# The last piece of the Fourier weight fold ahead of the last two gate blocks, and the output weights of the even layer split by GpSimd

## The chip, the cores and the metric

The kernel runs on one core of one Trainium2 chip. The metric is the device time of one launch in microseconds. Its matmuls run on PE (TensorE, with PEld for its weight loads), and DVE, ACT and POOL are VectorE, ScalarE and GpSimd. SP issues most of the DMAs, and POOL issues some.

## The reference

One inference step of a two-layer backbone over 1280 tokens of width 1024, 1024 latent and 256 context tokens. Cut to what the change touches:

```python
# layer 0 (even): two attention mixers (8 heads of 64 each) and a SiLU gate for each
qa, ka, va, ga, qb, kb, vb, gb = split_even(h @ w_in)
oa = attention over all latent and context keys
ob = attention over a window of +-128 tokens and the context keys, with a sink
x = x + gate * (concat([oa * silu(ga), ob * silu(gb)]) @ w_out)
# layer 1 (odd): Fourier mixing, also gated
u, g = split(modulate(rms_norm(x)) @ w_in1)
x = x + gate * ((real(fft2(u, axes=(positions, group channels))) * silu(g)) @ w_out1)
y = rms_norm(x)
```

The channel half of the Fourier transform of one group is a product with a fixed matrix. The kernel multiplies it into the odd layer's input weights instead of applying it to the tokens; this product of two weights is the *fold*, in four groups f0 to f3.

## The kernel before, in words

**Arithmetic.** The tokens are ten tiles of 128 (0 to 7 latent, 8 and 9 context). Each fp32 operand of a projection is held as a high and a low part of the type fp32r, high = the rounded value and low = value minus high, and a product is three matmuls (`mm3`). `split` makes the two parts: one engine copies the high part, another then subtracts. The letters "a", "d" and "p" in its arguments name ACT, DVE and POOL, and a longer string such as "pd" is a cycle.

**Stages.** First the modulation vectors, the normalised tokens and the folds f0 to f2; then the projections of layer 0; then attention, from about 240 us of the span to about 800; then the output projection of layer 0, the norm, and layer 1. Attention runs in units (tile, key group, head pair), which `attend` walks. One unit computes scores (`soft`: sC against context keys, sB against the window, sL against all latent keys), takes maxima on DVE, exponentials on ACT, transposes the probabilities on PE (pt), splits them with an ACT copy (L277) and a DVE subtraction (L1048), and multiplies by the values (`weigh`: av). When the last key group of a tile t is done, `totals` makes its softmax denominators (tt, stored in scd). Outputs go to DRAM (od).

**The filler.** A unit leaves PE idle while ACT and DVE work. So the rest of layer 0 is put into one queue of pieces with a cost each (`Filler`), and after each unit `attend` pumps as many pieces as the unit's budget pays for: 2.9 us for a unit of the windowed mixer. In the queue, by `ORDER`: the remaining q and k/v blocks, then the SiLU gate blocks g0 to g3. The last two of these are run together, by token group: ga40, ga50, ga60, ga70, then ga41 and so on up to ga72 (the digits are column block and token group). Between these pieces stand the splits of the output weights (`wout_next`), eight blocks of 128 rows, each in two halves: a load on SP (`sp.dma_start`, L1107) into a raw tile of the zone h, the high part by ACT (E_WO "a", L277), the low part by POOL and DVE in turn (L283), each 128x512. A half needs the raw tile until its low part is done; zone h has nine tiles, which the gates use too. After the gates come: the load of the fold f3 (two tiles of zone w, 512 KB each, and the fixed matrix, 256 KB), the loads of the first output projection's inputs (`load_to(0)`), the four fold pieces (wa30 to wa33: eight matmuls L559 each, into the one PSUM bank "g", out of it by an ACT copy, stored to wd by SP), and then the ten steps of the output projection (oz), each preceded by its loads. A gate block uses the same bank "g", and frees it when the tanh (L817) and the DVE operations behind it have read it.

**Inputs of the output projection.** `proj_in` loads od, gd (the stored gates), scd (denominators) and the residual x from POOL's own DMA queue while attention runs, and from SP's afterwards. It multiplies od, gd and scd together (L1221, L1222, on POOL while attention runs, on DVE afterwards) and splits the product (ACT, then DVE). After a step comes `proj_step`: the residual is added, the squares are summed by ACT (L1344), the token rows normalised (p, L1370) and transposed (eoE, L1274).

**Order.** The program text gives the dependences; the instructions of each engine are then laid out in the order of the framework's own timeline, so that a change in one place moves rows of every engine behind it. Only SP's order in the first phase is written by hand.

Of the kernel before, what the change touches and what calls it, by code (L numbers as in the profile page):

```python
# [24 lines left out]
UV = ("u",)  # L25
FILL_A, FILL_B, LAG_A, LAG_B = 4.4, 2.9, 1, 2
E_PH, E_OH, E_OL, E_WO = "a", "a", "d", "a"
# [30 lines left out]
FC, XF = 1.3, False  # L58
# [2 lines left out]
PAIRS = ((0, 4), (2, 6), (3, 7), (1, 5), (8, 9))  # L61
FILL_C, NLATE = 2.9, 8
E_FQ, E_GD = "d", "d"
ORDER = "qa0 qa1 kb0 qb0 qb1 g0 g1 g2 g3"
FLATE = "f3"
AT_B = "s"
AT_F = (0, 1, 2)
AT_N, AT_Z = (0, 0, 3, 0, 3, 2, 2, 2, 2, 2, 3, 3, 3), ("p", "pt", "q")
# [71 lines left out]
def hybrid_step(ctx: ExitStack, tc: tile.TileContext, I, O):  # L140
# [140 lines left out]
    def split(dst_h, dst_l, src, hc="a", lc="p"):  # L281
        copy("hi" + hc, hc, dst_h, src)
        pick("lo" + lc, lc).tensor_sub(dst_l, src, dst_h)  # L283


    def load_w(src, width=256, tags="w", gap=None, lc=E_WL, each=None, later=None):
        out = []
        for kp in range(2):
            hi = take(tags, (P, 4, width), F32R)
            lo = take(tags, (P, 4, width), F32R)  # L290
            for j in range(2):
                r0 = (kp * 4 + j * 2) * P
                if width <= 256:
                    raw = take("h", (P, 2, width))
                else:
                    raw = take(("p", "pt", "q", "w"), (P, 2, width))
                if gap is None:
                    sp.dma_start(raw.a, src[r0 : r0 + 2 * P, :].rearrange("(j p) f -> p j f", p=P))
                else:
                    gap(raw, r0)  # L300
                if each is not None:
                    each(raw, kp * 4 + 2 * j)

                def fin(raw=raw, hi=hi[:, 2 * j : 2 * j + 2, :], lo=lo[:, 2 * j : 2 * j + 2, :]):
                    split(hi, lo, raw.a, XE["wh"], lc)
                    drop(raw)

                if later is None:
                    fin()
                else:  # L310
                    later.append(fin)
            out.append((hi, lo))
        return out
# [11 lines left out]
    def w0cols(c0):  # L325
        return I["w_in0"][:, c0 : c0 + 256]
# [209 lines left out]
    def fold_load(g, parts=1):  # L536
        if "f" not in fold:
            fold["f"] = take("h", (P, 2, 256))
            sp.dma_start(fold["f"].a, I["fch"])
        wu = [take("w", (P, 1024)) for j in range(2)]  # L540
        for h in range(parts):
            cols = slice(h * (1024 // parts), (h + 1) * (1024 // parts))
            for j in range(2):
                sp.dma_start(wu[j][:, cols], I["wuT"][(2 * g + j) * P : (2 * g + j + 1) * P, cols])
        return wu
# [7 lines left out]
    def fold_piece(g, kb2, wu, first=False):  # L553
        f = fold["f"]
        acc = bank("t" if first else "g", f"wa{g}{kb2}")
        for i in range(2):
            c0 = (2 * kb2 + i) * P
            for j in range(2):
                pe.matmul(  # L559
                    acc[:, i * 256 : i * 256 + 256], wu[j][:, c0 : c0 + P], f[:, j, :], start=j == 0, stop=j == 1  # L560
                )
        if first:
            if kb2 % 2 == 0:
                early[g, kb2 // 2] = take("u", (P, 4, 256))
            wo = early[g, kb2 // 2][:, 2 * (kb2 % 2) : 2 * (kb2 % 2) + 2, :]
        else:
            wb = take("h", (P, 2, 256))
            wo = wb.a
        copy("wo", "a", wo, acc.rearrange("p (i f) -> p i f", i=2))
        if not first:  # L570
            fold_put(g, kb2 * 256, wo)
            drop(wb)
        if kb2 == 3:
            drop(*wu)
            fold["n"] = fold.get("n", 0) + 1
            if fold["n"] in (EF, 4):
                drop(f)
                del fold["f"]
# [265 lines left out]
    fl_ = Filler()  # L844
    fl_.depth = 9
    ws = {}
# [250 lines left out]
                after(u0)  # L1097
            fl_.pump(budget(un))

    def out_weights(src, ks, tags, lc="pd"):  # L1100
        out = []
        for k in ks:
            hi, lo = take(tags, (P, D), F32R), take(tags, (P, D), F32R)
            for hf in range(2):
                raw = take("h", (P, 512))
                sl = slice(hf * 512, hf * 512 + 512)
                sp.dma_start(raw.a, src[k * P : (k + 1) * P, sl])  # L1107
                split(hi[:, sl], lo[:, sl], raw.a, E_WO, lc)
                drop(raw)
            out.append((hi, lo))  # L1110
        return out
# [3 lines left out]
    wout = []  # L1115
    ws["qa0"] = wqa0

    def loader(nm):
        def fn():
            ws[nm] = load_w(w0cols(base[nm[:-1]] + 256 * int(nm[-1])))  # L1120
            return 0
        return fn
# [11 lines left out]

    def wout_next(n):
        for _ in range(n):
            fl_.add(0.0, lambda k=wk_left.popleft(): wout.extend(out_weights(I["w_out0"], (k,), UV)) or 0)

    for i, nm in enumerate(order[:-1]):
        j = int(nm[-1])  # L1140
        work = []
        if nm[0] == "q":
            m = "ab".index(nm[1])
            for t in range(0, NT, 2):
                if nm == "qa0" and t in (0, 2):
                    continue
                work.append((5.4, lambda t=t, nm=nm, m=m, j=j: q_pair(m, j, t, ws[nm], "g"), ("q", t, 2 * m + j)))
        elif nm == "kb0":
            for t in range(0, NT, 2):
                work.append((5.4, lambda t=t, nm=nm: kv_pair(1, t, ws[nm], "g"), ("kb", t)))  # L1150
        elif i < len(order) - 2:
            work += [gate_work(j, c, gi) for c in range(2) for gi in range(3)]
        if i > 0:
            fl_.add(0.0, loader(order[i + 1]))
        for w in work:
            fl_.add(*w)
        if i < len(order) - 2:
            fl_.add(0.0, releaser(nm))

    for gi in range(3):  # L1160
# [223 lines left out]
    def can_run(i, j):  # L1384
        r = pairs[i][j]

        def fn():
            if sum(len(spare[z]) for z in OB[0]) < NSP or i > EARLY:
                return False
            return all(finished.get(t, 99) + SPAN < clock[0] for t in USES[r])  # L1390
        return fn
# [5 lines left out]
    def load_to(n):  # L1397
        while loaded[0] <= min(n, 9):
            proj_load(*steps[loaded[0]])
            loaded[0] += 1  # L1400
        return 0


    def late_fold(nm):
        def fn():
            ws[nm] = fold_load(int(nm[1]))
            return 0
        return fn

    for n, nm in enumerate(FLATE.split()):  # L1410
        fl_.add(0.0, late_fold(nm))
        if n == 0:
            fl_.add(0.0, lambda: load_to(0), ready=can_run(0, 0))
        for k in range(4):
            fl_.add(FC, lambda k=k, nm=nm: fold_piece(int(nm[1]), k, ws[nm]))
    if not FLATE:
        fl_.add(0.0, lambda: load_to(0), ready=can_run(0, 0))
    for n, ij in enumerate(steps):
        if n == 8:
            fl_.add(0.0, lambda: wgs.append(load_w(I["w_g1"][:, 0:256], tags=BIG)) or 0)  # L1420
# [413 lines left out]
    hi, lo, xr = ins1  # L1834
# [133 lines left out]
```

## Time and profile before

| what | us |
|---|---|
| runs of the kernel, median (lowest to highest) | 1191.62 (1185.96 to 1196.26) |
| the profiled execution: span from its first to its last instruction | 1196.9 |
| PE busy in the span | 1159.1 |
| DVE busy | 834.5 |
| ACT busy | 577.1 |
| POOL busy | 286.0 |
| moved by DMA | 168.81 MB |

The profile is one execution, here one that took 5.3 us more than the median of the runs; everything between the first and the last instruction is in its span, and nothing is known of what lies around it. Rows of the waits give engine, operation and line, what ended the wait, and then total idle us, count, and median. In rows of the timeline the first number is the time in the span and the second the duration, and the brackets hold the idle time ahead and what ended it. The granted clock is the share of full clock that PE was given, 0.50 being half.

### The profile page before, as it was taken

What the parts mean: (1) busy time and instruction counts of PE and PEld (TensorE: products, weight loads), DVE (VectorE), ACT (ScalarE), POOL (GpSimd) and SP (SyncE); (2) the same over time, 40 slices, a digit from 0 to 9 for tenths busy, and PEclk for the clock granted to TensorE, in tenths of its full rate; (3) what the DMA queues carried; (4) which work ended last, traced back from release to release, by engine and by line L of the source; (5) the groups of instructions that cost most, each with busy time, mean ns of one, the idle gap of its engine ahead of it and who ended that gap; (6) DMA issues with size and microseconds to landing.
All of it is one profiled execution on the core that took longest, in us unless ns stands there. A gap on an engine that the chain in (4) does not pass through costs nothing.

```text
span 1196.9 us, 22002 instructions
## 1 busy us (share of the span) xinstructions
PE 1159.1 (97%) x8103; PEld 1037.9 (87%) x8103; DVE 834.5 (70%) x2006; ACT 577.1 (48%) x1159; POOL 286.0 (24%) x272
## 2 busy tenths in 40 slices
PE   8999999999999999999999989998999999999997
PEld 6788899999999998899888878886878888998886
DVE  2489778787777776678888867777755964367543
ACT  4442555555656655556676654532364225333211
POOL 2255644512222230011010035200212226200001
PEclk9999999999999999999999989998998999999999
DMA  9978512323532232444354477774214435364321
GB/s 327 365 257 272 160 59 69 89 77 113 148 89 78 76 95 84 100 120 116 83 148 105 131 223 203 232 224 160 85 45 136 147 115 167 109 186 150 141 105 54
DMA packets 130096, 168.81 MB, mean 141 GB/s; under 512 B 26298, under 2 KB 86454, under 8 KB 129988
## 3 DMA queue, kind: packets, MB, share of 16 engines
q1 hardware_dynamic: 127476, 158.74, 43.5%
q0 software_dynamic: 2368, 8.39, 2.3%
q8 instruction: 64, 1.05, 0.4%
q14 instruction: 44, 0.36, 0.1%
q10 hardware_dynamic: 144, 0.26, 0.1%
HBM read 123.19 MB, written 44.16 MB: 140 GB/s over the span
## 4 chain that ended last, share of the span: by engine, by line
PE 80%; DMA 9%; DVE 5%; ACT 2%; issue 2%; SPq 1%; POOL 1%; POOLq 0%; DVEq 0%; ACTq 0%
PE of L265 9%; PE q L265 8%; PE av L1051 8%; PE pt L1045 8%; PE ga L265 7%; PE sL L928 5%; PE u L265 5%; PE oz L265 4%; PE g1E L265 4%; PE g1O L265 4%; PE kv L265 3%; PE sC L928 2%; PE wa L559 2%; PE g1c L265 2%; DMA h<-i_w_out 2%
## 5 line engine op out<-in xcount | busy, mean ns | idle before, releaser
L277 ACT ACTIVATE pt<-pt 128x512 fp32r<-128x512 f32 (+1 forms) x265 | 146.8, 575 | 107.0 <-PE pt L1045 60.2
L1048 DVE TENSOR_TENSOR pt<-pt,pt 128x512 fp32r<-128x512 f32 (+1 forms) x264 | 170.8, 658 | 37.7 <-ACT pt L277 36.8
L1051 PE MATMUL av<-pt,u 128*128 128x256 f32 x1008 | 167.1, 289 | 0.7 <-ACT pt L277 0.7
L1045 PE MATMUL pt<-identr,p 128*128 128x128 f32 x1008 | 157.4, 273 | 1.1 <-ACT p L969 0.8
L265 PE MATMUL q<-w,u 128*128 128x256 f32 x960 | 143.9, 287 | 0.0
L1051 PEld LDWEIGHTS av<-pt,u 128*128 128x128 f32 x1008 | 138.9, 190 | 4.6 <-ACT pt L277 0.9
L265 PEld LDWEIGHTS q<-w,u 128*128 128x128 f32 x960 | 126.8, 188 | 4.9 <-issue 0.8
L1045 PEld LDWEIGHTS pt<-identr,p 128*128 128x128 f32 x1008 | 119.7, 141 | 8.0 <-ACT p L969 1.0
L969 ACT ACTIVATE p<-p,nm 128x1280 f32<-128x1280 f32 (+1 forms) x80 | 95.5, 1194 | 63.1 <-DVE p L962 62.8
L265 PE MATMUL ga<-u,w 128*128 128x512 f32 (+1 forms) x576 | 124.1, 360 | 0.8 <-DVE byp L1024 0.5
L265 PEld LDWEIGHTS ga<-u,w 128*128 128x128 f32 x576 | 93.6, 188 | 15.2 <-ACT pt L277 1.2
L283 POOL TENSOR_TENSOR w<-h,w 128x512 fp32r<-128x512 f32 x38 | 51.1, 1360 | 143.4 <-DVE w L279 115.0
L928 PE MATMUL sL<-u,q 128*128 128x512 f32 x256 | 82.4, 411 | 2.0 <-DMA q<-qd 2.0
L969 ACT ACTIVATE p<-p,NM 128x640 f32<-128x640 f32 (+2 forms) x80 | 59.2, 740 | 39.5 <-DVE p L962 39.4
L928 PE MATMUL sC<-u,q 128*128 128x256 f32 x320 | 61.8, 294 | 1.6 <-DMA q<-qd 1.0
L962 DVE TENSOR_SCALAR_CACHE_REDUCE p<-sL 128x512 f32<-128x512 f32 x64 | 43.9, 685 | 23.2 <-PE sL L928 14.2
L962 DVE TENSOR_SCALAR_CACHE_REDUCE p<-sL,nm 128x512 f32<-128x512 f32 x64 | 47.7, 745 | 13.7 <-PE sL L928 12.9
L265 PE MATMUL oz<-u,w 128*128 128x512 f32 x192 | 57.3, 403 | 0.0
L283 POOL TENSOR_TENSOR u<-h,u 128x512 fp32r<-128x512 f32 x16 | 20.6, 1293 | 138.0 <-ACT u L277 133.9
L928 PEld LDWEIGHTS sC<-u,q 128*128 128x128 f32 x320 | 48.8, 189 | 5.5 <-issue 1.1
L265 PE MATMUL oz<-u,u 128*128 128x512 f32 x160 | 48.7, 405 | 4.0 <-ACT u L277 2.5
L702 POOL TENSOR_TENSOR h<-h,rope 128x512 f32<-128x512 f32 (+1 forms) x18 | 21.9, 1214 | 126.4 <-ACT h L785 80.5
(728 smaller groups left out, 2569.8 us busy)
## 6 DMA issues: line engine op xcount, KB each, us to landing
q<-qd SPq DMA_DIRECT2D x80, 256.0 KB
h<-i_w_in SPq DMA_DIRECT2D x40, 256.0 KB
p<-i_ada_w SPq DMA_DIRECT2D x18, 512.0 KB
h<-i_w_out SPq DMA_DIRECT2D x32, 256.0 KB
pt<-i_ada_w SPq DMA_DIRECT2D x15, 512.0 KB
qd<-pt SPq DMA_DIRECT2D x20, 256.0 KB
q<-i_ada_w SPq DMA_DIRECT2D x9, 512.0 KB
qd<-q SPq DMA_DIRECT2D x18, 256.0 KB
```

What stands on the lines that cost most here:

```text
L265: pe.matmul(out, a, b, start=i == 0, stop=i == n - 1)
L277: act.activation(out, in_, AF.Copy)
L283: pick("lo" + lc, lc).tensor_sub(dst_l, src, dst_h)
L559: pe.matmul(acc[:, i * 256 : i * 256 + 256], wu[j][:, c0 : c0 + P], f[:, j, :], start=j == 0, stop=j == 1)
L702: pick("rope", XE["rope"]).tensor_mul(t1.rearrange("p t h (b c) -> p t (h b) c", b=2), y.rearrange("p t h (b c) -> p t (h b) c", b=2), cb)
L928: pe.matmul(ps, q_at(q, s, hc), keys, start=s == 0, stop=s == 1)
L962: dve.tensor_scalar(p[i][:, end[i] : end[i] + n], ps, sign, last[i], op0=ALU.mult, op1=ALU.min, accum_out=c)
L969: act.activation(p[i][:, 0 : end[i]], p[i][:, 0 : end[i]], AF.Exp, bias=last[i], scale=-1.0, accum_out=SU[:, t, hd + i, 0:1],)
L1045: pe.transpose(tp[:, jj * 256 + i * P : jj * 256 + i * P + P], p[i][:, off : off + P], ident)
L1048: dve.tensor_sub(pt[:, 1, 0:n], tp[:, 0:n], pt[:, 0, 0:n])
L1051: pe.matmul(acc, vv, pt[:, s, jj * 256 : jj * 256 + 256], start=c + jj + s == 0, stop=c + jj == nt - 1 and s == 1,)
```

## The change

Two things. First, f3 becomes an entry of `ORDER`, ahead of g2: its load and its four pieces stand between the gate blocks g1 and g2, and no longer between the last gates and the output projection. `load_to(0)` then stands directly ahead of the steps. Second, the splits of the output weights in the filler are made by POOL alone: the high part by a POOL copy in place of ACT's, the low part always by POOL in place of POOL and DVE in turn.

```diff
-ORDER = "qa0 qa1 kb0 qb0 qb1 g0 g1 g2 g3"
-FLATE = "f3"
+ORDER = "qa0 qa1 kb0 qb0 qb1 g0 g1 f3 g2 g3"
...
-    def out_weights(src, ks, tags, lc="pd"):
+    def out_weights(src, ks, tags, lc="pd", hc=E_WO):
...
-                split(hi[:, sl], lo[:, sl], raw.a, E_WO, lc)
+                split(hi[:, sl], lo[:, sl], raw.a, hc, lc)
...
     def loader(nm):
         def fn():
+            if nm[0] == "f":
+                ws[nm] = fold_load(int(nm[1]))
+                return 0
...
-            fl_.add(0.0, lambda k=wk_left.popleft(): wout.extend(out_weights(I["w_out0"], (k,), UV)) or 0)
+            fl_.add(0.0, lambda k=wk_left.popleft(): wout.extend(out_weights(I["w_out0"], (k,), UV, "p", "p")) or 0)
...
+        elif nm[0] == "f":
+            work += [(FC, lambda k=k, nm=nm, j=j: fold_piece(j, k, ws[nm])) for k in range(4)]
...
-        if i < len(order) - 2:
+        if i < len(order) - 2 and nm[0] != "f":
             fl_.add(0.0, releaser(nm))
...
-    def late_fold(nm):
-        def fn():
-            ws[nm] = fold_load(int(nm[1]))
-            return 0
-        return fn
-
-    for n, nm in enumerate(FLATE.split()):
-        fl_.add(0.0, late_fold(nm))
-        if n == 0:
-            fl_.add(0.0, lambda: load_to(0), ready=can_run(0, 0))
-        for k in range(4):
-            fl_.add(FC, lambda k=k, nm=nm: fold_piece(int(nm[1]), k, ws[nm]))
-    if not FLATE:
-        fl_.add(0.0, lambda: load_to(0), ready=can_run(0, 0))
+    fl_.add(0.0, lambda: load_to(0), ready=can_run(0, 0))
```

In the rows below an instruction is given as output<-inputs with the partitions and elements of its output; `ga72` is the last gate, `h` tiles hold raw weights and tanh values, `u` and `w` tiles hold split weights.

ACT around the last gate, before:

```order
L1060 ACTIVATE e891_9048<-av1_20_9015 64x256
L277 ACTIVATE pt901_9136<-pt1_212_9131 128x512
L277 ACTIVATE pt902_9146<-pt1_214_9143 128x256
L969 ACTIVATE p934_9321,SU_105<-p934_9321,NM_106 128x256
L277 ACTIVATE u919_9276<-h921_9278 128x512
L817 ACTIVATE h917_9268<-ga72_9243 128x256
L277 ACTIVATE pt913_9220<-pt7_300_9215 128x512
```

The same place after the change, where lines are one less:

```order
L276 ACTIVATE pt926_9313<-pt7_312_9308 128x512
L1059 ACTIVATE e910_9191<-av7_30_9166 64x256
L968 ACTIVATE p943_9402,SU_105<-p943_9402,NM_106 128x640
L276 ACTIVATE pt945_9431<-pt8_200_9426 128x512
L1029 ACTIVATE e929_9334<-tt7_9332 16x128
L968 ACTIVATE p948_9444,SU_105<-p948_9444,NM_106 128x640
L816 ACTIVATE h930_9363<-ga72_9338 128x256
```

The row `u919<-h921`, the high part of the last half of the output weights, stood directly ahead of the tanh of ga72; no row of this kind is left on ACT, and the tiles of attention around the gate are later ones (7 and 8 in place of 1 and 7). The high parts are now on POOL, whose rows behind the last gates are these:

```order
L278 CAST u920_9271<-h922_9273 128x512
L1236 DMA w942_9398<-i_xp 128x1024
L282 TENSOR_TENSOR u933_9372<-h935_9377,u932_9371 128x512
L282 TENSOR_TENSOR u921_9272<-h922_9273,u920_9271 128x512
L278 CAST u932_9371<-h934_9373 128x512
L1219 DMA u937_9385<-od_72 128x1024
L1222 DMA w960_9539<-gd_73 128x1024
L282 TENSOR_TENSOR u933_9372<-h934_9373,u932_9371 128x512
L1224 DMA u939_9388<-scd_77 64x1024 x2
L1222 DMA u938_9387<-gd_73 128x1024
```

A copy on POOL is printed CAST. The loads of the first projection's inputs (od, scd, gd) now stand between or behind the last halves of the output weights in POOL's own order.

PE between the last gate and the first output projection (oz00), before:

```order
L1051 MATMUL av8_20_9425<-pt945_9431,u438_4475 128x256 x4
L559 MATMUL wa33_9390<-h923_9286,w924_9288 128x256
L559 MATMUL wa33_9390<-h923_9286,w925_9289 128x256
L559 MATMUL wa33_9390<-h923_9286,w924_9288 128x256
L559 MATMUL wa33_9390<-h923_9286,w925_9289 128x256
L928 MATMUL sC9_20_9485<-u438_4475,q944_9420 128x256 x2
L928 MATMUL sC5_30_9692<-u687_7079,q953_9494 128x256 x2
L928 MATMUL sC9_21_9629<-u438_4475,q944_9420 128x256 x2
L1045 MATMUL pt6_310_9639<-identr_85,p948_9444 128x128 x4
L1051 MATMUL av8_21_9465<-pt949_9471,u438_4475 128x256 x4
L265 MATMUL oz00_9552<-u826_8504,w930_9305 128x512
```

After the change:

```order
L927 MATMUL sC5_31_9736<-u682_7065,q953_9494 128x256 x2
L999 MATMUL sB5_310_9743<-u680_7063,q953_9494 128x384 x2
L999 MATMUL sB5_311_9748<-u680_7063,q953_9494 128x384 x2
L1050 MATMUL av6_31_9638<-pt975_9644,u682_7065 128x256 x4
L1050 MATMUL av6_31_9638<-pt976_9656,u681_7064 128x256 x4
L1050 MATMUL av6_31_9638<-pt977_9666,u681_7064 128x256 x2
L927 MATMUL sC5_31_9736<-u682_7065,q953_9494 128x256 x2
L1044 MATMUL pt5_300_9875<-identr_85,p981_9691 128x128
L927 MATMUL sC1_30_9850<-u682_7065,q982_9711 128x256 x2
L264 MATMUL oz00_9552<-u847_8681,w940_9394 128x512
```

The four fold pieces are gone from this stretch; 20 sC, 10 sB, 33 pt and 36 av matmuls stand in it now, and 20 sC, 8 sB, 38 pt and 34 av stood in it before beside the fold.

ACT where attention ends, before:

```order
L1060 ACTIVATE e1038_10230<-av8_31_10217 64x256
L1030 ACTIVATE e1047_10296<-tt9_10294 16x128
L1060 ACTIVATE e1042_10260<-av9_30_10247 64x256
L1344 ACTIVATE h1084_10558,ss1_104<-pt1059_10328 128x1024
L1060 ACTIVATE e1045_10280<-av9_31_10267 64x256
L277 ACTIVATE u1070_10420<-p1067_10411 128x1024
```

After the change:

```order
L1029 ACTIVATE e1047_10296<-tt9_10294 16x128
L1360 ACTIVATE p1063_10398<-w1007_9925,r11y_10395 128x1024
L1059 ACTIVATE e1042_10260<-av9_30_10247 64x256
L1059 ACTIVATE e1045_10280<-av9_31_10267 64x256
L276 ACTIVATE u1070_10420<-p1067_10411 128x1024
L1380 ACTIVATE pt1066_10406<-p1063_10398 1x1024
L1348 ACTIVATE h1084_10558,ss1_104<-pt1059_10328 128x1024
```

The split of the last projection input (u1070) stood behind the sum of squares h1084 and stands ahead of it now. On PE, 51 oz matmuls and two av rows stood between the totals of the last tile (tt9) and the first eoE; now 87 and two. From tt8 on it is 93 before and 120 after. On SP, the load of the last half of the output weights stood behind the stored gates of ga62 and stands behind those of ga52 now.

## The prediction

> **What bounds the kernel now.** I read the page first: busy time, then the clock row.
>
> ```profile
> PE 1159.1 (97%) x8103; PEld 1037.9 (87%) x8103; DVE 834.5 (70%) x2006; ACT 577.1 (48%) x1159; POOL 286.0 (24%) x272
> PEclk9999999999999999999999989998998999999999
> ```
>
> PE is busy for 97% of the span, so only two things shorten it: fewer PE instructions, which the change doesn't bring, or less idle PE and less time at a low clock. The idle time is 1196.9 - 1159.1 = 37.8 us in all. The clock row has three dips, each in one or two slices of 30 us, all where attention ends and the output projection begins. So the next view is that of PE's waits between 600 and 830 us (total us, count, median):
>
> ```profile
> PE wa L559 <- ACT pt L277: 4.5, 1, 4.5
> PE oz L265 <- ACT u L277: 2.5, 1, 2.5
> PE eoE L1274 <- DVE p L1370: 2.0, 1, 2.0
> ```
>
> Then the windows, where a row has length, busy us of PE, PEld, DVE, ACT and POOL, the granted clock, DMA share and GB/s:
>
> ```profile
> 660.00:670.00 10.00, 8.71 (x59) 7.30 (x58) 9.17 (x26) 7.24 (x17) 1.30 (x1) 1.00 0.38 114
> 690.00:700.00 10.00, 5.49 (x36) 4.94 (x35) 2.76 (x9) 3.35 (x9) 3.09 (x6) 0.87 0.73 241
> 700.00:710.00 10.00, 10.00 (x56) 9.23 (x56) 7.51 (x24) 5.37 (x13) 5.34 (x4) 0.79 0.89 249
> 810.00:820.00 10.00, 5.57 (x24) 3.94 (x23) 8.47 (x10) 3.02 (x6) 0.31 (x1) 0.84 0.60 174
> 820.00:830.00 10.00, 10.00 (x37) 7.95 (x37) 5.17 (x7) 2.12 (x2) 0.00 (x0) 0.81 0.55 184
> 892.00:899.00 7.00, 5.00 (x25) 3.43 (x23) 2.45 (x8) 5.07 (x14) 2.56 (x2) 0.99 0.25 75
> 899.00:905.00 6.00, 5.76 (x25) 5.29 (x26) 4.86 (x17) 3.97 (x12) 1.28 (x1) 0.50 0.13 44
> ```
>
> Two stalls stand out. In 690:700 PE is idle for 4.5 us, and the clock loses (1 - 0.87) x 10 + (1 - 0.79) x 10 = 3.4 us over that window and the next, in which PE is busy without a gap. In 810:820 PE is idle for 4.4 us, and the clock loses 1.6 + 1.9 = 3.5. Each stall thus costs 7.9 us, nearly half of it afterwards. The timeline of the first shows its cause:
>
> ```profile
> 690.53 0.38 SPq L1107 DMA_DIRECT2D h<-i_w_out  x1
> 696.75 0.63 ACT L277 ACTIVATE u<-h 128x512 fp32r<-128x512 f32 x1 [6.60 <-DMA h<-i_w_out]
> 697.29 0.36 ACT L817 ACTIVATE h<-ga 128x256 f32<-128x256 f32 x1
> 698.27 3.75 PE L559 MATMUL wa<-h,w 128*128 128x256 f32 x8 [4.51 <-ACT pt L277]
> ```
>
> The load of the last half of the output weights goes out at 690.53 and lands at 696.7. ACT stands for 6.6 us in front of its high part. Behind it in ACT's order are the tanh of ga72, which frees the bank that wa30 needs, and the pt copies of attention: PE has neither filler nor attention. The eight matmuls of the fold piece, at the clock of 0.50, take 3.75, so 1.9 at full clock. In the second stall PE waits for two things in a row:
>
> ```profile
> 815.78 0.55 PE L1274 MATMUL eoE<-identr,p 128*128 128x128 f32 x3 [1.96 <-DVE p L1370]
> 816.36 1.06 ACT L1344 ACTIVATE h<-pt 128x1024 bf16<-128x1024 f32 x1 [4.86 <-DVE pt L1244]
> 817.68 1.04 ACT L277 ACTIVATE u<-p 128x1024 fp32r<-128x1024 f32 x1
> 818.78 1.22 PE L265 MATMUL oz<-u,u 128*128 128x512 f32 x2 [2.45 <-ACT u L277]
> ```
>
> The last projection input is split by ACT at 817.68, behind a sum of squares that waits for a DVE result until 816.36, and PE's next oz needs it.
>
> **The change part by part.**
>
> *ACT no longer splits the output weights.*
>
> ```profile
> ACT u L277 <- DMA h<-i_w_out: 16.9, 8, 6.6
> SPq L1107 <- POOL u L283: 4.5, 3, 2.1
> ```
>
> ACT waits for such loads 16.9 us in eight places in 600:720 (first row), and only POOL waits for them now. PE suffered in two of the places. Stall 1 goes with its half clock: 4.5 + 3.4 = **-7.9**. The window 660:670, where PE is idle for 1.3, has the same kind of wait ahead of ACT: **-1.3**. What is late next? POOL, and behind it the first projection's input and SP; both are costed below.
>
> *POOL does the whole split.* These rows give the durations here and in the next steps (mean ns behind the total):
>
> ```profile
> L283 POOL TENSOR_TENSOR u<-h,u 128x512 fp32r<-128x512 f32 x16 | 20.6, 1293 | 138.0 <-ACT u L277 133.9 <-PE sB L1000 4.2
> L350 POOL MEMSET u<- 128x1024 f32 x2 | 1.8, 956 | 11.9 <-PE oz L265 11.9
> L277 ACT ACTIVATE u<-h 128x512 fp32r<-128x512 f32 x18 | 11.0, 629 | 22.3 <-DMA h<-i_w_out 16.9 <-PE oz L265 2.6 <-PE ga L265 1.5
> L283 DVE TENSOR_TENSOR u<-h,u 128x512 fp32r<-128x512 f32 x8 | 5.5, 683 | 1.9 <-ACT u L277 1.9
> L1048 DVE TENSOR_TENSOR pt<-pt,pt 128x512 fp32r<-128x512 f32 x65 | 43.8, 679 | 3.4 <-ACT pt L277 3.3
> L962 DVE TENSOR_SCALAR_CACHE_REDUCE p<-sC,nsink 128x256 f32<-128x256 f32 x67 | 31.1, 471 | 2.2 <-PE sC L928 2.0
> L962 DVE TENSOR_SCALAR_CACHE_REDUCE p<-p,nm 128x384 f32<-128x384 f32 x40 | 23.8, 599 | 0.1
> L1006 DVE SCALAR_TENSOR_TENSOR p<-sB,maskf 128x384 f32<-128x384 f32 x40 | 21.4, 546 | 4.7 <-PE sB L1000 4.7
> L1062 DVE TENSOR_TENSOR e<-av,e 64x256 f32<-64x256 f32 x37 | 15.2, 410 | 11.4 <-ACT e L1060 8.1 <-DMA od<-e 3.2
> ```
>
> ACT is relieved of 16 x 0.629 = 10.1 us and DVE of 8 x 0.683 = 5.5; neither bounds the stretch, so 0 by themselves. The POOL copy is not in this trace. Below, half of a fill of 1024 columns, 0.956 / 2 = 0.48; above, the subtraction of 512 columns, 1.29. I take 0.8, between them, since a copy reads one operand where the fill reads none and the subtraction two. Sixteen halves make 16 x (0.8 + 1.293) = 33 us (28 to 41) on POOL over the gate blocks of some 70 us, 48% of the time: hidden, **0**. The first projection's input waits for the last half 0.2 us longer (2.1 in place of 0.63 + 1.293), which is nothing beside the rest. If the cover is gone, that is rival C.
>
> The Trainium skill (GPSIMD Engine Reference, 4.1 Engine selection) says that elementwise work belongs on VectorE, two-input operations being about twice as slow on GpSimd and one-input ones about line rate. The trace agrees for the subtraction, 1.293 against 0.683. By this rule the copy would lie nearer to the lower bound, 28 us on POOL, and the sum stays; it is the objection on which rival C rests.
>
> *The fold is moved.* Its four pieces are 4 x 1.9 = 7.6 us of PE, done either way, as are its DMAs (two of 512 KB, one of 256 KB, four stores) and four ACT copies; SP issues them twelve gate pieces earlier, ahead of the loads of g2, which no wait of PE above names. **0**; if g2's first matmul came late it would be one more stall like stall 1. But the pieces were cover where they stood. Between ga72 and oz00 PE now has 20 sC, 10 sB, 33 pt and 36 av, by these rows of the chain of waits (duration, then count; the last has oz):
>
> ```profile
> 625.20 0.35 PE sB L1000 x2
> 625.55 0.44 PE pt L1045 x4
> 625.99 0.24 PE sC L928 x2
> 626.23 1.18 PE av L1051 x10
> 764.64 5.58 PE oz L265 x24
> ```
>
> That is 20 x 0.12 + 10 x 0.175 + 33 x 0.11 + 36 x 0.118 = 12.0, and with oz00's 5.6 it is 17.6 us. DVE has for these units 7 x 0.546 (mask), 6 x 0.599 and 9 x 0.471 (maxima), 8 x 0.679 and 2 x 0.41 (pt; the narrow ones put at the last row's price, which has as many columns), 5 x 0.41, and the low part of the projection's input, two of 0.683: 21.3. If DVE is the slower here PE idles 21.3 - 17.6 = 3.7. The input itself comes by this chain:
>
> ```profile
> 700.28 0.54 POOL L1218 DMA_DIRECT2D w<-gd  x1
> 705.41 2.37 POOL L1221 TENSOR_TENSOR u<-u,u 128x1024 f32<-128x1024 f32 x1 [4.58 <-DMA u<-gd]
> 713.72 1.05 ACT L277 ACTIVATE w<-u 128x1024 fp32r<-128x1024 f32 x1
> 742.81 9.33 DMA w<-gd
> ```
>
> Issue to first product 705.41 - 700.28 = 5.1, two products of 2.37, the high part 1.05, the low part 1.4: 12.3, or 16.5 if the load takes 9.3 as in the last row. PE's 12.0 us of attention in the same time cover 12.3 barely. Bounds: 0 (DVE runs ahead, since ACT no longer holds it up) and 3.7 + 3.4 + 4.2 = 11.3 (DVE bound, half clock, late load). I take **+3.7**, nearer to the first because attention there no longer stands behind a blocked ACT.
>
> *Attention ends earlier against the projection.* In the new order 36 more oz stand between the last totals and the first eoE, 36 x 5.58 / 24 = 8.4 us, and 27 more from tt8 on, 6.3 us; the split of the last input stands ahead of the sum of squares. The wait of 2.0 + 2.5 is shorter than either. The work is not new, it is taken from the stretch before. Stall 2 goes: **-7.9**. Bounds: -7.9 and 0, where 0 means that the transfers behind the last totals land that much later.
>
> *The sum.* -7.9 - 1.3 + 3.7 - 7.9 = -13.4: the profiled execution's 1196.9 would be 1183.5. Against the runs it is 5.3 us above the median of 1191.62. Taken off the median, 13.4 gives 1178.2, if the stalls are as long in a median run. I take half of the excess to be stall time that a median run doesn't have, so 1191.62 - 13.4 + 2.65 = **1180.9 us**, 0.9% less.
>
> **The rivals.** *A2: the gap behind the last gate also trips the clock.* The third dip of the clock follows only 7.00 - 5.00 = 2.0 us of idle PE, in pieces, in 892:899, and 899:905 runs at 0.50. A gap of 3.7 in pieces would do so too: +3.4, 1184.3 us. Against it: 660:670 has 1.3 idle at 1.00. The Trainium skill (TensorE: Matmul & The Clock Gate, Part 1: The HAM clock gate) gives half clock after an idle window of about 3.4 us. The trace agrees for the two stalls; the third dip has less idle time than that and contradicts it. By the rule a gap in pieces would cost no clock, which is my forecast.
>
> *B: stall 2 stays.* The transfers behind the totals, or the residual chain to p, set its time whatever stands before. For it: loads of 9.3 us exist. Against it: 8.4 us of oz are added as cover. 1180.9 + 7.9 = 1188.8.
>
> *D: the cover holds.* DVE runs ahead and oz00 comes on time: 1180.9 - 3.7 = 1177.2, and 1173.8 if the third dip goes as well. For it: ACT loses 10.1 us and DVE 5.5 in just this stretch.
>
> *C, slower: POOL holds the raw tiles, and SP's loads of q stand behind them.* Two blocks are queued at once, four halves, 4 x 2.1 = 8.4 us of POOL. SP then waits in front of the next load of output weights, as it already did three times for POOL (4.5 us, second fence of this part), and the q loads behind it in SP's one queue come late. A unit has 2 sC and 2 sB pairs, ten pt and ten av, so 3.4 us of PE by the rows above, and 2.9 of filler: q is asked for a unit or two, 6.3 to 12.6 us, ahead. It decides from a delay of SP above 6.3. Then PE stops as in stall 1, at two such bursts: 2 x 7.9 = 15.8, and attention ends no earlier, so stall 2 stays as well: 1180.9 + 15.8 + 7.9 = 1204.6. Against it: SP waited for POOL 2.1 at a time when POOL had half as many halves' work.
>
> **How the numbers follow.** Forecast 0.42, A2 0.15, B 0.20, D 0.13, C 0.10. The range goes from 1169, below D with stalls as long as in the profile, to 1198, above B with a clock loss, short of C. A measurement here tells about 1% from no change: 1179.7 and 1203.5. Faster by more: D whole, two fifths of the forecast (its choice of half the excess lies just above the bound), a little of A2 and B: 0.37. Slower: C's greater part and a few mishaps, 0.10. The rest 0.53.
>
> **What would show it.** In the profile after: no ACT wait for the output weights, and no PE idle of over 2 us before ga72's tanh; CAST rows of 0.5 to 1.3 us on POOL; the fold pieces near g2 at 1.9; PE idle of 3 to 4 us between ga72 and oz00 with DVE the releaser; no wait of oz and eoE in 790:820, and one clock dip in place of three. I am wrong if PE waits for q behind SP's queue (C), if the gap shows a clock of 0.50 (A2), or if oz still waits for the last input (B).

## The result, and the profile after

| | before | after |
|---|---|---|
| median of 12 runs, us (lowest to highest) | 1193.98 (1185.96 to 1199.9) | 1203.8 (1196.95 to 1208.49) |
| ratio, 95% interval | | 1.0088 (1.0069 to 1.0107) |
| span of the profiled execution | 1196.9 | 1203.1 |

The change makes the kernel about 10 us slower (9.8 between the medians, 10.5 by the ratio). In the page of the changed kernel PE is busy for 2.5 us less than before, and idle for 8.7 more (1203.1 - 1156.6 = 46.5 against 37.8); the clock row has one dip in place of three, in the slice that begins at about 722 us:

```profile
PE 1156.6 (96%) x8103; PEld 1035.1 (86%) x8103; DVE 828.4 (69%) x1994; ACT 571.1 (47%) x1147; POOL 306.4 (25%) x296
PEclk9999999999999999999999998999999999999999
```

PE's waits of the changed kernel between 680 and 745 us (total, count, longest) have a new first row:

```profile
PE av L1050 <- DVE e L1061: 9.7, 2, 9.3
PE sC L927 <- DMA q<-qd: 2.5, 1, 2.5
PE pt L1044 <- DVE pt L1047: 1.3, 1, 1.3
```

A value product (av) waits 9.3 us for DVE, and DVE has not been busy. The chain of waits of the changed kernel shows what DVE waited for (start, duration, what):

```profile
712.29 12.29 DMA od<-e
724.59 0.03 issue
724.61 0.02 DVEq L1061
724.63 0.04 issue
724.68 0.43 DVE e L1061
725.11 0.14 issue
725.24 2.06 PE av L1050 x8
```

A store of one attention output, at most 64 KB, was issued at 712.29 and landed 12.3 us later. Its tile is one of four in zone e; DVE may not write the next output into it until it has gone, the value products behind that output have no bank, and PE stops. The rows of POOL in the same kernel show the same store from the other side:

```profile
706.26 0.58 POOL L1219 DMA_DIRECT2D u<-od  x1
709.69 0.55 POOL L1222 DMA_DIRECT2D u<-gd  x1
...
724.89 0.55 POOL L1219 DMA_DIRECT2D w<-od  x1 [11.50 <-DMA od<-e]
725.45 2.38 POOL L1225 TENSOR_TENSOR u<-u,u 128x1024 f32<-128x1024 f32 x1
727.92 2.38 POOL L1226 TENSOR_TENSOR u<-u,u 128x1024 f32<-128x1024 f32 x1
```

POOL stood 11.5 us in front of the load of the second input's od, which reads what that store writes, and the products of the *first* input, whose last operand was asked for at 709.69 and landed 10.9 us later, stand behind it. So the input of oz00 came late as well. In four windows of the changed kernel the share of the DMA engines (last column but one) says why a small store took so long:

```profile
705.00:710.00 5.00, 5.00 (x45) 4.97 (x44) 3.98 (x15) 3.03 (x8) 4.27 (x7) 1.00 0.70 154
710.00:715.00 5.00, 3.53 (x25) 2.65 (x23) 4.03 (x16) 4.83 (x16) 1.27 (x3) 1.00 1.04 307
715.00:720.00 5.00, 0.44 (x2) 0.20 (x2) 0.42 (x1) 0.00 (x0) 0.00 (x0) 0.79 1.06 220
720.00:725.00 5.00, 0.00 (x0) 0.00 (x0) 0.32 (x1) 0.00 (x0) 0.11 (x1) 0.50 1.06 234
```

From 710 to 725 all 16 engines are in use without a pause, while PE, DVE, ACT and POOL come to a stand. Call the stretch from the end of the last gate to oz00 the *hole*. One window over the hole, and one over what follows up to the first eoE, for the changed kernel:

```profile
706.90:733.60 26.70, 15.09 (x102) 13.29 (x101) 13.97 (x46) 10.73 (x28) 12.96 (x13) 0.81 0.86 213
733.60:821.50 87.90, 85.97 (x444) 71.64 (x443) 68.54 (x138) 38.27 (x84) 18.86 (x18) 1.00 0.73 214
```

The same two for the kernel before:

```profile
690.90:718.10 27.20, 21.74 (x130) 19.82 (x130) 16.75 (x52) 15.85 (x37) 9.31 (x10) 0.87 0.82 233
718.10:815.80 97.70, 92.89 (x496) 77.94 (x494) 73.29 (x158) 41.27 (x93) 22.86 (x20) 1.00 0.69 212
```

The four fold pieces are out of the hole, and it is as long as it was: 26.7 against 27.2. PE is idle in it for 26.7 - 15.1 = 11.6 us in place of 5.5. The clock loss over the whole hole is (1 - 0.81) x 26.7 = 5.1 in place of 3.5, but most of the 5.1 lies in idle time, where it costs nothing: when PE works again, from 725.2 to 733.6, the clock is 0.83, a loss of 1.4, against 3.0 before (0.52 from 698.3 to 704.5). What was taken out of it is paid in full where it now stands, ahead of g2.

Two theories. **Transfers:** the hole takes as long as its transfers take, and PE's work in it is free, so the moved fold was free and now costs 7.6 us. **GpSimd:** the splits on POOL hold back its loads until they all go out at once, and that makes the stop. A third, weaker one, is that any new order moves stalls by a per cent.

### The profile page after: what moved, and what is told of

Read it like the earlier page. It is cut to its first block, busy times and chain, and to the rows that moved or that the text cites. A ratio compares the mean times of both kernels' runs of the same rounds, so it can differ in the third digit from the quotient of the medians.

```text
span 1203.1 us, 21992 instructions
## 1 busy us (share of the span) xinstructions
PE 1156.6 (96%) x8103; PEld 1035.1 (86%) x8103; DVE 828.4 (69%) x1994; ACT 571.1 (47%) x1147; POOL 306.4 (25%) x296
## 4 chain that ended last, share of the span: by engine, by line
PE 79%; DMA 9%; DVE 7%; ACT 2%; issue 1%; SPq 1%; POOL 0%; POOLq 0%; DVEq 0%; ACTq 0%
PE of L264 9%; PE av L1050 9%; PE ga L264 9%; PE q L264 8%; PE pt L1044 8%; PE oz L264 6%; PE sL L927 5%; PE u L264 5%; PE g1E L264 3%; PE kv L264 3%; PE sC L927 3%; PE g1O L264 3%; PE g1c L264 1%; DMA od<-e 1%; PE sB L999 1%
## 5 line engine op out<-in xcount | busy, mean ns | idle before, releaser
L282 POOL TENSOR_TENSOR w<-h,w 128x512 fp32r<-128x512 f32 x40 | 53.6, 1355 | 92.7 <-DVE w L278 55.1
L264 PE MATMUL oz<-u,w 128*128 128x512 f32 x192 | 51.9, 400 | 0.2 <-DVE w L282 0.2
L264 PE MATMUL of<-u,u 128*128 128x512 f32 x150 | 50.3, 394 | 0.0
```

What stands on the lines that cost most here:

```text
L264: pe.matmul(out, a, b, start=i == 0, stop=i == n - 1)
```

## The experiments

Each ratio below is to runs of the kernel before that were made beside the experiment's own.

**Each half alone.** e1 moves the fold only, e2 moves the splits to POOL only.

```diff
# e1, on the changed kernel
-... out_weights(I["w_out0"], (k,), UV, "p", "p") ...
+... out_weights(I["w_out0"], (k,), UV) ...
# e2, on the changed kernel
-ORDER = "qa0 qa1 kb0 qb0 qb1 g0 g1 f3 g2 g3"
+ORDER = "qa0 qa1 kb0 qb0 qb1 g0 g1 g2 g3"
+    fl_.add(0.0, lambda: ws.__setitem__("f3", fold_load(3)) or 0)
     fl_.add(0.0, lambda: load_to(0), ready=can_run(0, 0))
+    for k in range(4):
+        fl_.add(FC, lambda k=k: fold_piece(3, k, ws["f3"]))
```

> The changed kernel with the output weights split as before (high part by ACT, low by POOL and DVE in turn): the fold's move alone. Theory (burst): the move takes away the four fold pieces that stood between the loads of the first and of the second projection input, so both go out at once, the stores of attention's outputs stand behind them and the four e tiles run out; then this kernel shows the long stop of PE behind the last gate as well: ratio to before 1.005 to 1.012. Rival (GpSimd): the splits on GpSimd hold back its queue and with it the loads; then this kernel has no such stop and stands at 0.99 to 1.00. Rival (order): any change of order brings as much; then it lies anywhere from 0.99 to 1.01 with stops in other places.

> The kernel before with the output weights split by GpSimd alone and the last fold where it was: the other half of the change. Theory (burst): the fold pieces still part the loads of the two inputs, stall 1 of the kernel before (4.5 idle and 3.4 of clock) is gone since ACT waits for no load of output weights: ratio 0.99 to 0.997. Rival (GpSimd): the stop of 9 us behind the last gate is here: 1.005 to 1.012.

Measured: e1 1.0057 (1.0039 to 1.0075), e2 1.0011 (0.9995 to 1.0026). The fold's move alone makes the kernel slower; POOL's splits alone change nothing that can be told. But e2 did not bring the gain that was expected of it either: its hole has 5.4 us of idle PE, now in front of loads of q. The holes of e1 and then e2:

```profile
705.70:727.90 22.20, 16.84 (x111) 14.76 (x109) 17.86 (x57) 14.46 (x38) 10.24 (x10) 0.92 0.89 245
```

```profile
688.10:714.40 26.30, 20.93 (x133) 19.53 (x132) 19.95 (x56) 15.66 (x38) 10.79 (x12) 0.94 0.93 225
```

e2 and the changed kernel differ only in the fold's place. Their holes are equally long, 26.3 and 26.7, with 20.9 and 15.1 us of busy PE. That is the first theory's picture. In e1 the long stop of 9.3 is not there (its largest wait in the hole is 3.6 for q), so the size of that stop is not the fold's alone.

**Are the stalls the same in another execution?** The two kernels once more, unchanged, for a second profile of each.

> The kernel before once more, for a second profile. If its two stalls (4.5 and 4.4 us idle, 3.4 of clock each) belong to its order of work, they stand here at the same instructions, within 1 us; if they depend on when transfers happen to land, one of them is shorter or at another instruction, and the span is nearer to the median of 1191 to 1194.

> The changed kernel once more. Theory (transfers): the store behind the last gate lands 10 us or more after its issue again, and PE stops for 8 to 10 us in the same place. If it was an accident of that execution, it lands in under 7.

Second profiles: spans of 1189.1 and 1201.0. In the changed kernel the stop is there again, in its chain of waits (first row) and its DVE rows (second):

```profile
710.00 12.10 DMA od<-e
```

```profile
722.19 0.42 DVE L1061 TENSOR_TENSOR e<-av,e 64x256 f32<-64x256 f32 x1 [9.04 <-DMA od<-e]
```

In the kernel before, stall 1 is *not* there again. The same instructions of its second execution, SP's load and ACT's rows:

```profile
689.10 0.38 SPq L1107 DMA_DIRECT2D h<-i_w_out  x1
```

```profile
692.50 0.63 ACT L277 ACTIVATE u<-h 128x512 fp32r<-128x512 f32 x1 [2.33 <-DMA h<-i_w_out]
693.03 0.36 ACT L817 ACTIVATE h<-ga 128x256 f32<-128x256 f32 x1
```

The load took 692.50 - 689.10 = 3.4 us, not 6.2, ACT waited 2.3, not 6.6, and PE's fold piece behind it waited 0.24, not 4.5, as PE's rows show:

```profile
694.01 1.97 PE L559 MATMUL wa<-h,w 128*128 128x256 f32 x8 [0.24 <-ACT pt L277]
```

The second stall is there again in part: PE waits 2.5 us for the split of the last input as before, and 0.4 in place of 2.0 at eoE. The holes of the second profiles, before and then after:

```profile
690.90:714.20 23.30, 20.43 (x130) 18.93 (x129) 17.12 (x49) 16.18 (x37) 10.34 (x12) 0.93 0.89 258
```

```profile
704.10:731.50 27.40, 15.72 (x100) 13.98 (x99) 14.19 (x46) 10.69 (x28) 13.53 (x14) 0.75 0.85 209
```

**Keep the second input's loads out of the burst.** e3 puts them behind the first step in the queue; e5 makes them wait for the tiles of the input before.

```diff
# e3
-        if n < 9:
+        if 0 < n < 9:
...
         fl_.add(7.7, lambda ij=ij: proj_step(*ij))
+        if n == 0:
+            fl_.add(0.0, lambda: load_to(1), ready=can_run(*steps[1]))
# e5: take() gives the tile that came free last, while newest[0] is set
+            newest[0] = 1 <= loaded[0] <= 4
             proj_load(*steps[loaded[0]])
+            newest[0] = False
```

> The changed kernel with the loads of the second projection input put behind the first projection step in place of ahead of it. Theory (burst): the output store after ga72 lands in 4 to 7 us in place of 12.3, the stop of 9.3 us and its half clock go (about 14 us), and the second step may wait some 3 us for its input: ratio to before 0.995 to 1.001. If the stop stays (rival GpSimd, or the load of q that the burst is made of too): 1.006 to 1.01.

> The changed kernel in which the loads for projection inputs 2 to 5 take the tiles that came free last, those of the input before, so that they cannot go out until its products are made. The arithmetic is the same. In e3 the loads of the second input were still issued in the old place, since nothing made them wait. Theory (transfers): in the 12 us behind the last gate all 16 DMA engines are busy, PE has only attention there, and attention waits for its stores and for q; with some 1 MB less of 4 MB asked for at once the stop of 9 us shortens to 5 or 6, and later steps may wait some us for their inputs: ratio to before 1.002 to 1.009. Rival (order): the stop stays at 9 or moves.

Measured: e3 1.0141 (1.0119 to 1.0163), e5 1.0178 (1.0143 to 1.0213); both are slower than anything that was expected, and neither tells the two theories apart as meant. In e3 the loads went out in the old place, because their order comes from the framework's timeline and nothing made them wait; the stop of 8.9 us stayed (store: 12.0 us). In e5 the loads that waited made room for others, as much passed through the hole as in the changed kernel (5.7 MB), the stop was 8.8, and the steps behind it waited for their inputs (12 us idle between oz00 and eoE). But e5 answers another question. POOL's rows there have the first product, and the next load of od:

```profile
717.92 2.33 POOL L1230 TENSOR_TENSOR u<-u,u 128x1024 f32<-128x1024 f32 x1 [9.22 <-DMA u<-gd]
732.02 0.57 POOL L1224 DMA_DIRECT2D u<-od  x1 [7.77 <-DVE w L287]
```

No load of od stands ahead of the first products here; they begin when their gd has landed, 7.5 us earlier than in the changed kernel, and PE still stops for 8.8 us behind a store that takes 11.9. So POOL's place in front of the second od load is not what makes the stop.

**More output tiles.** e4 lets attention's outputs use zone h as well, from the last split of the output weights on.

```diff
-        lo_sb = take("e", (64, 2, P))
-        os_ = take("e", (64, 2, P))
+        ez = "e" if len(wout) < 8 else ("e", "h")
+        lo_sb = take(ez, (64, 2, P))
+        os_ = take(ez, (64, 2, P))
```

> The changed kernel in which attention's output tiles may also be taken from zone h once the output weights are split (up to 13 tiles in place of 4). The loads stay as they are. Theory (burst with four e tiles as what stops DVE): the store still takes about 12 us, but DVE and PE do not wait for it; the stop of 9.3 us and its half clock go, 10 to 14 us: ratio to before 0.996 to 1.001. If the transfers themselves are the bound, PE waits for q or for the projection's input in the same place for 5 us or more: 1.004 to 1.01.

Measured: 1.0099 (1.0079 to 1.0118), the second outcome. PE's waits of e4 between 700 and 740 us:

```profile
PE sC L927 <- DMA q<-qd: 8.7, 1, 8.7
PE av L1050 <- DVE h L1062: 0.8, 1, 0.8
```

DVE's wait for a tile is gone (0.8 left), and PE stops as long as before, now for a load of q in the same queue. The four tiles were only the first thing to run out.

**Fewer transfers.** e6 leaves out the gating and the division by the totals for the first four projection inputs, with their loads; POOL's two products stay.

```diff
+        few = gate is not None and r in PAIRS[0] + PAIRS[1]
+        if few:
+            flush_held()
+            ol = take(OB[0], (P, 8, P))
+            ld.dma_start(ol.a, src[r])
+            for h in range(2):
+                pick("pm", XE["pm"]).tensor_mul(ol.a, ol.a, ol.a)
-        if gate is not None:
+        elif gate is not None:
```

> The changed kernel with part of the computation left out: the first four projection inputs are not gated and not divided by their totals; their loads of gates and totals are left out (1 MB each), and GpSimd's two products are kept, made of the attention output with itself. Theory (transfers): the loads of the stretch behind the last gate fall from some 4 MB to 3 or less; the DMA engines are saturated for 8 us or less in place of 12, the stop of 9.3 us falls to 0 to 4: ratio to before 0.995 to 1.002. Rival (the four e tiles, or GpSimd's products on the chain): the stop stays at 7 us or more, 1.006 or above.

Measured: 1.0053 (1.0035 to 1.0071), less of a gain than expected. The hole of e6:

```profile
706.50:723.20 16.70, 11.07 (x68) 9.64 (x67) 12.25 (x32) 9.73 (x25) 12.91 (x12) 0.80 0.87 251
```

It is 10 us shorter than the changed kernel's, with the same splits on POOL and as many products. That fits the transfers, but is not a clean test of them: with the loads, POOL's waits for gd and scd are gone too, and its first product begins at 711.83 in place of 725.45. The idle time fell from 11.6 to 5.6 us, the largest wait for DVE from 9.3 to 2.7. The time fell by only 4 us: the attention that no longer fits into the shorter hole comes later (92.5 us from oz00 to eoE in place of 87.9).

**Other cover.** e7 puts the last two gates behind the first input's loads; e8 the fold as well; e9 is e8 with the splits as in the kernel before. In all three the first input's loads also no longer wait until a number of tiles are free, only until their tokens' attention is done.

```diff
# e7, on the changed kernel
-            fl_.add(*gate_work(jj, c, gi))
+            if gi == 2 and n > 1:
+                tail.append(gate_work(jj, c, gi))
+            else:
+                fl_.add(*gate_work(jj, c, gi))
...
     fl_.add(0.0, lambda: load_to(0), ready=...)
+    for wk_ in tail:
+        fl_.add(*wk_)
# e8, on e7: no f3 in ORDER, and behind these gates
+    fl_.add(0.0, lambda: ws.__setitem__("f3", fold_load(3)) or 0)
+    for k in range(4):
+        fl_.add(FC, lambda k=k: fold_piece(3, k, ws["f3"]))
# e9, on e8
-... out_weights(I["w_out0"], (k,), UV, "p", "p") ...
+... out_weights(I["w_out0"], (k,), UV) ...
```

> The changed kernel with the last two gate pieces (context tokens, 2.8 us of PE each) put behind the loads of the first projection input in place of ahead of them: other cover where the fold was. Theory (transfers take a fixed time, and what counts is the work that PE has beside them): 5.6 us of PE come back into the stretch, the stop shrinks by about as much and its half clock by 1.7: ratio to before 1.002 to 1.005. If the cover is not what was lost (rival GpSimd or order): 1.008 as the change.

> As e7, with the fold late as well, behind these two gates: 5.6 and 7.6 us of PE beside the loads, and 1.25 MB more to load and store there. Theory: PE has 13 us of cover in the saturated stretch, as much as the loads take; no stop above 3 us there: ratio to before 0.993 to 0.999, better than e2's 1.001. If the fold's own transfers lengthen the stretch by as much: 1.000 to 1.003.

> As e8 (the last two gates and the fold behind the first input's loads), with the output weights split as in the kernel before, by ACT and by POOL and DVE in turn. Theory (transfers): who splits matters little once the stretch has cover: within 0.003 of e8's 1.0009, so 0.998 to 1.004. Rival (ACT blocked in front of the loads is a cost of its own, 7.9 us as in the prediction): 1.006 or more.

Measured: e7 1.0062 (1.0037 to 1.0086), just above what was expected, with the rival's 1.008 inside its interval; e8 1.0009 (0.999 to 1.0029), its second outcome, no better than the kernel before; e9 1.0074 (1.0045 to 1.0102), the rival's outcome. e7 and e8 differ in the fold's place alone, and again the hole is as long with the fold (21.7) as without it (21.4), and the early fold 0.53% slower. The hole of e8 has 2.9 us of idle PE, that of e9 is 6 us longer:

```profile
693.70:715.40 21.70, 18.75 (x129) 17.54 (x128) 17.11 (x54) 15.88 (x39) 6.92 (x8) 0.99 0.90 262
```

```profile
698.60:726.00 27.40, 21.49 (x127) 19.51 (x127) 16.34 (x50) 15.69 (x38) 5.59 (x8) 0.88 0.74 215
```

These holes begin when the first input's loads have long been asked for: directly ahead of it, e8 has another wait of 4.3 us for q. From the first load of od to oz00 PE is idle for 7.2 us in e8 and for 6.0 in e7, so the longer stops of e7 are not there: of the 6.1 us that PE is idle more in its profile, 4.1 lie between ga00 and these loads, and 2.9 between oz00 and eoE. In e9 ACT waits up to 7.2 us for a load of output weights, in a row of its waits between 600 and 730 us:

```profile
ACT u L276 <- DMA h<-i_w_out: 17.8, 8, 7.2
```

So the split by ACT costs 0.65% between e8 and e9; it does so in this order, and did not in the kernel before. That ACT's waits are the way is not shown: PE's own waits of e9 from 660 to 726 end with DVE's e (5.9 in two), the fold's own load (3.4) and q (2.5).

**All holes in one table.** Length, PE busy and clock are from the window of each hole; idle is length minus busy, clock loss is (1 - clock) x length with the idle time in it, so the two must not be added, and MB is the rate times the length. In e7 to e9 the hole begins behind the two gates that were moved, so their lengths compare with each other only.

| kernel | fold | splits | hole us | idle | clock loss | MB | ratio |
|---|---|---|---|---|---|---|---|
| before | late | ACT | 27.2 | 5.5 | 3.5 | 6.3 | 1 |
| before, second profile | late | ACT | 23.3 | 2.9 | 1.6 | 6.0 | 1 |
| e2 | late | POOL | 26.3 | 5.4 | 1.6 | 5.9 | 1.0011 |
| e8 | late, gates behind | POOL | 21.7 | 2.9 | 0.2 | 5.7 | 1.0009 |
| e9 | late, gates behind | ACT | 27.4 | 5.9 | 3.3 | 5.9 | 1.0074 |
| e1 | early | ACT | 22.2 | 5.4 | 1.8 | 5.4 | 1.0057 |
| e7 | early, gates behind | POOL | 21.4 | 6.0 | 5.1 | 4.7 | 1.0062 |
| e6, loads left out | early | POOL | 16.7 | 5.6 | 3.3 | 4.2 | 1.0053 |
| e3 | early | POOL | 26.2 | 11.2 | 5.2 | 5.7 | 1.0141 |
| e4, more tiles | early | POOL | 27.3 | 10.8 | 5.2 | 5.7 | 1.0099 |
| e5 | early | POOL | 25.2 | 10.9 | 5.0 | 5.7 | 1.0178 |
| after | early | POOL | 26.7 | 11.6 | 5.1 | 5.7 | 1.0088 |
| after, second profile | early | POOL | 27.4 | 11.7 | 6.9 | 5.7 | 1.0088 |

Where the arithmetic is whole and the gates stand in front, 5.4 to 6.3 MB pass through the hole at 209 to 258 GB/s, in 22 to 27 us, with the fold or without. All kernels with an early fold are slower by 0.5% or more; with a late one two of three are not. The split between ACT and POOL has no fixed sign: no difference with the fold late (e2 against before), 0.3% for ACT with the fold early (e1 against after, intervals that touch), 0.65% for POOL with the gates behind (e8 against e9).

## Why the prediction was wrong, point by point

The prediction said 1180.9 us and a gain of 13.4 on the profiled execution; measured is a loss of about 10. Take the second profiles, 1189.1 and 1201.0, +11.9: -0.7 up to the first gate (ga00), +16.3 from there to ga40, with which g2 begins behind the fold's new place, -2.4 on to the end of the gates, +4.1 in the hole, -6.6 from oz00 to eoE, and +1.2 behind. The windows of the second of these stages, before and then after:

```profile
448.70:571.10 122.40, 122.40 (x821) 111.66 (x820) 88.95 (x262) 72.11 (x149) 11.78 (x11) 1.00 0.40 105
```

```profile
448.00:586.70 138.70, 136.78 (x913) 124.73 (x912) 98.75 (x296) 84.58 (x179) 10.88 (x10) 1.00 0.43 115
```

PE's 16.3 us more are 7.6 of fold, 1.9 of idle and 6.8 of attention that was pulled forward; the attention comes back as -6.6 behind oz00. The fold does not come back: the hole, out of which it was taken, is no shorter. It is 4.1 longer here and was 0.5 shorter in the first profiles, and two executions of the kernel before differ by 3.9 there. PE runs the same 8103 matmuls in both kernels, so the loss must show as idle time or low clock. Of the 10.6 us that it is idle more in all (44.4 in place of 33.8), 8.8 are in the hole, and 1.9 are a stop ahead of the fold's new place that the kernel before does not have.

- **Stall 1, -7.9: wrong.** It was the price of one execution. In the second profile the load landed in 3.4 us and PE was idle for 2.9 us in the whole hole. And the wait was not ACT's order at bottom: with the splits on POOL (e2) ACT waits for no such load, and PE stands idle for 5.4 us of the hole in front of q. The prediction's question, what is late next, was put to POOL and SP, not to the transfers, although its own rows had the DMA share at 0.73 and 0.89 around the stall.
- **The window at 660, -1.3: not found.** From the fold's new place to the end of the gates the idle time is 2.1 before and 1.9 after in the second profiles.
- **POOL's splits, 0: nearly right.** The copy that was put at 0.8 between 0.48 and 1.29 is in the POOL rows of the changed kernel:

```profile
L278 POOL CAST u<-h 128x512 fp32r<-128x512 f32 x16 | 9.7, 613 | 87.0 <-DMA h<-i_w_out 45.9 <-PE ga L264 41.1
```

With its 0.613 us the splits take 16 x (0.613 + 1.293) = 30.5 us. They were hidden. In the changed kernel POOL asks for the first input's od 0.6 us ahead of the last gate's end, in place of 1.7 before; in e2, with the same splits, it is 2.3 ahead, so that the splits delay this load is not shown.
- **The moved fold, 0 and +3.7: this is the step that failed.** Its 7.6 us of PE were put at 0 because they are done either way. They came back as 6 to 9 us in each of three pairs that differ in the fold's place alone: before and e1 (0.57%), e2 and the changed kernel (0.77%), e8 and e7 (0.53%). The gap that was left, +3.7, was sized by DVE's work and by a chain of loads whose durations came from a time when fewer of them were under way; even its upper bound, 11.3, was below the 11.6 us of idle PE that the hole shows. The 3.7 also counts oz00's own 5.6 us as PE's cover for the input that oz00 waits for; without them it is 21.3 - 12.0 = 9.3. That DVE would be the releaser came true, but by luck: it was idle for half of the hole (14.0 busy of 26.7) and stood for a store. The work between ga72 and oz00 was about as counted, 12.0 predicted, 15.1 - 1.4 = 13.7 found. What was missed is that the stretch already had a bound that is no engine, that PE's work there was nearly free, and that attention itself (its stores, its q) stands in the same queues.
- **Stall 2, -7.9: gone in part, and not worth it.** Both waits are gone, and 3.8 us of oz waiting for DVE (L1247) stand in their place. From oz00 to the last gate matmul of layer 1, idle and clock loss by the windows are 16.6 in the first profile before, 11.8 in the second, 11.7 and 12.1 after: a gain only against the worse execution.
- **Half of the profile's excess as stall time: too little.** The second execution is 7.8 us shorter, and nearly all of that is in three stretches with the same work: 3.9 in the hole, 1.8 up to eoE and 2.2 behind. And the excess itself was 7, not 5.3: it was taken between a span and a time, and in every run the time is 1.7 to 1.8 us above the span.

Two readings were off. The last number in the rows of waits is the longest wait, not the median, which changes no sum. And stall 2 does not have the one idle time above 3.4 us that the prediction takes from it: PE is idle there in pieces of 1.96 and 2.45, and the clock falls at about 816.8, within the second (0.84 over 810:820).

Of the rivals, A2 was right that the gap trips the clock (half clock for 10.2 us in the first profile, 13.7 in the second, most of it beside an idle PE). C named almost the measured time by another way: SP's wait for POOL was 4.4 us once, and the q that came late (2.5 us, ahead of the last gate) is not the long stop. The right rival, a stretch bound by its transfers, was not among them.

Shown by runs: the early fold costs 6 to 9 us by itself (the three pairs); with POOL's splits the hole is as long without the fold as with it (e2 and the changed kernel, e8 and e7); the tiles of zone e are not the cause of the stop (e4), nor is POOL's place in front of the od load (e5); and stall 1 does not recur (r1). With ACT's splits the hole did get shorter, to 22.2 in e1 from 27.2 and 23.3, so the fold was not wholly free there. The loss shows in the hole in the changed kernel, but in e7 mostly ahead of it and behind it. Argued only: that the transfers by themselves set the hole's length. It fits the share of the DMA engines, the wait that moved from DVE to q in e4, and the shorter hole of e6, which takes away waits of POOL as well. Open is why the stop is 9 us long in the changed kernel and not in e1; the later start of POOL's od load fits, but no run isolates it. Open is also by what way the split by ACT costs 0.65% in e9 and nothing in the kernel before.

## What to carry to other kernels

Before work is moved out of a stretch, ask what sets that stretch's length. Here the DMA engines were in use for 0.82 to 0.93 of the hole with the late fold (kernel before, e2), PE's 7.6 us of fold in it cost little or nothing, and they became a cost where they were put. A stall that is to be removed is priced from two profiled executions, not from one. When its wait ends with a transfer, ask who is next in line for a transfer: here it was DVE for a tile, PE for q, POOL for its load.

## What the runs showed of the hardware

A store of 64 KB or less took 12.3 and 12.1 us in the two profiles of the changed kernel, while the 16 DMA engines were in use throughout, and a load of 256 KB took 3.4 us in one execution and 6.2 in another of the same kernel. While the share stood at 1.04 to 1.06 in the changed kernel, the rate was between 220 and 307 GB/s: use is not rate. By the clock of the windows, the half clock came in stretches of about 3.4, 6.8, 10.2 and 13.7 us, and one of 3.4 followed 2.6 us of idle PE in the second profile of the kernel before. POOL copied 128x512 fp32 values in 0.61 us and subtracted two such tiles in 1.3.
